# Splitting the next output's weights ahead of the finished output's epilogue in a split-precision GEMM, with other PSUM banks and another mix of side work for one projection

## The chip, the core and the metric

The kernel runs on one core of a Trainium2 chip. The metric is the device time of one execution in microseconds (us), lower is better. Of several runs the median counts. A core has a tensor engine (PE, its weight loads are listed as PEld), a vector engine (DVE), a scalar engine (ACT), GpSimd (POOL) and a sync engine (SP) that here only issues transfers. Each has its own instruction stream, and they meet at semaphores.

## The reference, cut to what matters

The reference is a two-layer backbone over 256 latent tokens with 256 context tokens ahead of them, 1024 features wide, in fp32. Layer 0 mixes tokens with a Conformer convolution, layer 1 with a bidirectional chunkwise mLSTM. Each mixer is followed by a squared-ReLU MLP, and each sub-layer ends in a layer norm of the scaled stream plus the gated result.

```python
def sq_relu_mlp(u, w1, w2):
    return jnp.square(jax.nn.relu(u @ w1)) @ w2

def conformer_conv(u, rows, w_pw1, b_pw1, w_dw, b_dw, ln_g, ln_b, w_pw2, b_pw2):
    a = u @ w_pw1 + b_pw1
    a = a[..., :CONV_DIM] * jax.nn.sigmoid(a[..., CONV_DIM:])
    ...
    a = jax.nn.silu(layer_norm(a + b_dw, ln_g, ln_b))
    return a @ w_pw2 + b_pw2

def mlstm_features(u, w_up, w_conv, b_conv, w_q, w_k, w_v, w_gate, b_gate, w_o, b_o):
    up = u @ w_up
    xm, z = up[..., :MLSTM_INNER], up[..., MLSTM_INNER:]
    xc = jax.nn.silu(dwconv(xm, w_conv) + b_conv)
    q, k, v = xc @ w_q, xc @ w_k, xm @ w_v
    ...
```

Only latents need z, the gate half of the up projection: 16 outputs of 128 features by 256 tokens.

## The kernel before

Activations lie feature-major: a tile holds 128 features by 512 tokens, context in the first 256 columns (LO) and latents in the last 256 (HI). An fp32 product is built from two fp32r parts of each operand. For each 128x1024 block of weights, which is one output of 128 features (over 1024 input features), `split_w` makes the high part `wh` on ACT (a CAST at L154) and the low part `wl` on DVE (a subtraction at L155). `mm3` then issues three matmuls per block of 128 input features: wh by the high part of the activations (L177), wh by the low part (L180) and wl by the high part (L181), 24 per output. There are four buffers each of `wh` and `wl`, and three raw buffers (L148 to L151) that SP fills with 1 MB loads, two blocks in each.

`gemm_steps` (L209) is the loop over outputs for most projections: pw1 of the Conformer, most of both MLPs, up_x and up_z of the mLSTM, and others. Outputs come in groups of two that share a raw buffer. With `ko`, the first `ko` outputs are interleaved over the eight blocks of input features, since their activations arrive one by one. For the rest, a group takes both its PSUM banks at once, and then for each output splits the weights, issues the matmuls, calls the epilogue `epi`, and yields so that a caller may put other work between. PSUM has three banks with tag "mm", two "ln", one "fl" and two "cv".

The order in which the text issues instructions is not the final one. A scheduler sorts them by their dependences, the pools' buffers and its own estimates, with the text's order as priority, and writes one fixed stream for each engine. ACT's stream also holds the issues of several transfers to DRAM.

Three callers matter below. The first is pw1, whose epilogue `pw1_epi` (L648 to L660) makes a sigmoid on ACT (gate outputs) or a product on DVE (L655), four transposes on PE (L658) and a copy. During pw1, DVE also reduces rows of the modulation weights (the ISA instructions at L379, the products L766 and L768), and the Conformer's convolution runs in `spectral`: transforms on PE (L675, L680) into two "mm" banks, four products each on DVE (L690, L691), inverse transforms (L701) into a "cv" bank, and L708 and L709 behind them.

The second is z. Its epilogue `z_epi` (L1011 to L1015) is a sigmoid on ACT (L1013), a product on DVE that reads the bank too (L1014), and the issue of a transfer to `zs_dr` on ACT's stream (L1015). The outputs are interleaved with two side generators, one step per output: `u1_half(0)` makes the context half of the normalised activations `u` in eight steps (DVE L493, L494 and L516, ACT L515), and `rows` makes token-major rows of the latents in four (DVE L1029 into two `E` buffers, PE transposes L1035, ACT copies L1037). The `E` buffers, four in all, also hold z's epilogue results until their transfers are done.

The third is the v projection of the mLSTM after up_x, in which matmuls of v (weights wv) stand beside the folding of the gate weights: L812 multiplies raw wqT tiles straight from their raw buffers, so both kinds of loads go through the same three raw buffers and SP's stream.

Of the kernel before, what the change touches and what calls it, by code (L numbers as in the profile page):

```python
# [17 lines left out]
DT = D // P  # L18
# [4 lines left out]
C = 256  # L23
# [49 lines left out]
def hybrid_kernel(ctx: ExitStack, tc: tile.TileContext, xT, vecs_d, rows_d, wdw_d, ada0_w, ada_w, adar_w, wg_d, pw1a, pw1, pw2, w1_0, w2_0,  # L73
# [132 lines left out]
        for _ in gemm_steps(*a, **k):  # L206
            pass

    def gemm_steps(w_ap, groups, rhs, n, epi, ko=0, pre=None, mm=mm3):  # L209


        if isinstance(rhs, dict):
            parts = [(LO, rhs[0]), (HI, rhs[1])]
        else:
            parts = [(slice(0, n), rhs)]
        kh_n = len(parts[0][1]) // 8
        groups = list(groups)
        pre = pre or {}
        raws = {}
        if ko:  # L220
            ws, pss = [], []
            for m in range(ko):
                g = groups[m // 2]
                if m not in pre:
                    if g not in raws:
                        raws[g] = raw_load(w_ap[g, 0])
                    pre[m] = split_w(raws[g][:, (m % 2) * 1024:(m % 2 + 1) * 1024])
                ws.append(pre[m])
                pss.append(psum("mm" if m < 3 else "cv")[:, :n])
            for kt in range(8):  # L230
                for m in range(ko):
                    mm3(pss[m], *kcol(ws[m], kt), *rhs[kt], kt == 0, kt == 7)
            for m in range(ko):
                epi(m, pss[m])
        for gi, g in enumerate(groups):
            if 2 * gi + 1 < ko:
                continue
            ms = [m for m in (0, 1) if 2 * gi + m >= ko]
            pss = {m: psum()[:, :n] for m in ms}
            for kh in range(kh_n):  # L240
                raw = raws.get(g)
                for m in ms:
                    w = pre.get((g, kh, m))
                    if w is None:
                        if raw is None:
                            raw = raw_load(w_ap[g, kh])
                        w = split_w(raw[:, m * 1024:(m + 1) * 1024])
                    for sl, r in parts:
                        for kt in range(8):
                            mm(pss[m][:, sl], *kcol(w, kt), *r[kh * 8 + kt], kh == 0 and kt == 0,  # L250
                                kh == kh_n - 1 and kt == 7)
                    if kh == kh_n - 1:
                        epi(gi * 2 + m, pss[m])
                    yield

    def gemm2(*a, **k):
        for _ in gemm2_steps(*a, **k):
# [640 lines left out]
    side = silu(1)  # L898
# [5 lines left out]
    def mlp(w1, w2, uu, res, n, g2, feed, hmake, after, each1=None, each=None, keep=None, pre=None):  # L904

        def part(c):
            hid = {}

            def e1(m, ps, s=None, sl=slice(0, n)):
                r, q = tmp("E")[:, :ps.shape[-1]], tmp("E")[:, :ps.shape[-1]]  # L910
                nc.scalar.activation(r, ps, AF.Relu)
                nc.vector.tensor_tensor(q, r, r, op=ALU.mult)
                if m not in hid:
                    if n == T:
                        hid[m] = hmake(F32R), hmake(F32R)
                    else:
                        t = hmake(F32R)
                        hid[m] = t[:, :n], t[:, n:2 * n]
                split(hid[m][0][:, sl], hid[m][1][:, sl], q)
                if each1:  # L920
                    each1(c, m, s)

            groups = range(4 * c, 4 * c + 4)
            if keep and c == 0:
                gemm2(w1, groups[:3], uu, HALVES, e1, keep, ko=3)
                gemm(w1, groups[3:], uu, n, lambda m, ps: e1(m + 6, ps))
            else:
                gemm(w1, groups, uu, n, e1, ko=0 if c else 3 + Z.pre4 if pre else 3, pre=pre if c == 0 else None)
            after(c)

            def e2(m, ps, s=None, sl=slice(0, n)):
                for s_, g, sl_ in g2:
                    if s is None or s == s_:
                        p_ = ps if s is not None else ps[:, sl_]
                        nc.vector.scalar_tensor_tensor(res[m][:, sl_], p_, g[:, m:m + 1], res[m][:, sl_],
                                                       op0=ALU.mult, op1=ALU.add)
                if c == 3:
                    feed(m, s)
                if each:
                    each(c, m, s)  # L940

            hs = [hid[i] for i in range(8)]
            if keep and c == 3:
                gemm2(w2[c], range(4), hs, HALVES[::-1], e2, keep)
            else:
                gemm(w2[c], range(4), hs, n, e2, ko=Z.kw2)

        for c in range(4):
            part(c)
# [89 lines left out]

    side = u1_half(0)  # L1040
    side2 = rows()
    for i, _ in enumerate(gemm_steps(up_z, range(8), [(h_[:, HI], l_[:, HI]) for h_, l_ in u1], C, z_epi, ko=3)):
        next(side if i < DT else side2, None)
    for s_ in (side, side2):
        for _ in s_:
            pass
# [721 lines left out]
```

## Time and profile before

| what | value |
|---|---|
| runs | 1692.59, 1693.88, 1698.11 us, median 1693.88 |
| profiled execution | 1694.68 us |
| span of its trace | 1693.0 us, so 1.68 us lie around it |
| PE busy | 1661.1 us (98% of the span) |
| DVE busy | 1092.0 us (65%) |
| ACT busy | 745.7 us (44%) |
| POOL busy | 33.4 us (2%) |
| mean granted TensorE clock | 0.995 |

Rows of the timeline give the start in the span, the duration, the engine, the line, the operation, output and input; a bracket at the end holds the idle time before the instruction and what ended it. ACTq and SPq rows are issues of transfers. A row with "x3" stands for three instructions in a run. A row of stretches gives, for each engine, busy time and the number of instructions, then the granted clock of PE, the DMA engines' busy share and GB/s. Durations of PE matmuls overlap, so the time that an output takes is read from the starts.

### The profile page before, as it was taken

To read this page: it belongs to the slowest core of one execution; us is meant where nothing else is said; L and a number is where in the kernel's file an instruction comes from. 1 tells how busy PE (TensorE), PEld (TensorE's weight loads), DVE (VectorE), ACT (ScalarE), POOL (GpSimd) and SP (SyncE) were. 2 spreads that over 40 slices of the span, in tenths; PEclk is the share of its full clock that TensorE was granted. 3 is DMA by queue.
4 is the path that set the end of the run, shared out by engine and by line. 5 is a ranking of instruction groups with operands and counts; after the bars stand their busy time and mean duration, and the time that the engine had idled before them with its cause. 6 is when DMAs were issued, how large, how long until landed. Compare 5 with 4: busy or idle time off the path is not lost.

```text
span 1693.0 us, 22721 instructions
## 1 busy us (share of the span) xinstructions
PE 1661.1 (98%) x8853; PEld 1366.3 (81%) x8853; DVE 1092.0 (65%) x1964; ACT 745.7 (44%) x1206; POOL 33.4 (2%) x84
## 2 busy tenths in 40 slices
PE   8998999999999999999999999999999999999998
PEld 5754997888888998876688899888877878888886
DVE  7995897876666776763132543453387786678765
ACT  3322763232324465542232532442376674555652
POOL 0000000000000000000000000000011110000000
PEclk9999999999999999999999999999999999999999
DMA  9534216565554054568653642344355555645651
GB/s 386 210 130 160 102 57 225 199 222 199 199 195 178 26 183 158 190 217 274 239 191 101 219 150 100 104 171 144 119 187 198 187 188 212 242 172 218 240 186 47
DMA packets 60668, 301.60 MB, mean 178 GB/s; under 512 B 6066, under 2 KB 20946, under 8 KB 27152
## 3 DMA queue, kind: packets, MB, share of 16 engines
q1 hardware_dynamic: 42832, 285.44, 46.7%
q10 hardware_dynamic: 17728, 14.70, 2.7%
q8 instruction: 70, 1.15, 0.3%
q14 instruction: 38, 0.31, 0.1%
HBM read 284.37 MB, written 15.75 MB: 177 GB/s over the span
## 4 chain that ended last, share of the span: by engine, by line
PE 91%; DVE 5%; ACT 2%; issue 1%; DMA 1%; POOL 0%; SPq 0%; DVEq 0%; ACTq 0%; POOLq 0%
PE mm L177 17%; PE mm L180 17%; PE mm L181 17%; PE mm L192 4%; PE mm L187 3%; PE mm L185 3%; PE mm L1591 3%; PE mm L186 3%; PE mm L196 2%; PE cv L187 2%; PE cv L186 2%; PE cv L185 2%; PE mm L1592 2%; DVE wl L155 1%; PE fl L812 1%; PE ln L177 1%
## 5 line engine op out<-in xcount | busy, mean ns | idle before, releaser
L155 DVE TENSOR_TENSOR wl<-raw,wh 128x1024 fp32r<-128x1024 f32 x346 | 421.8, 1223 | 306.4 <-ACT wh L154 303.3
L154 ACT CAST wh<-raw 128x1024 fp32r<-128x1024 f32 x346 | 360.4, 1050 | 483.4 <-PE mm L180 286.3
L180 PE MATMUL mm<-u,wh 128*128 128x512 f32 (+1 forms) x848 | 301.8, 357 | 1.0 <-DVE u L525 0.6
L177 PE MATMUL mm<-u,wh 128*128 128x512 f32 (+1 forms) x720 | 253.6, 355 | 3.8 <-DVE E L1014 3.2
L181 PE MATMUL mm<-u,wl 128*128 128x512 f32 (+1 forms) x720 | 250.5, 350 | 0.5 <-DVE wl L155 0.5
L180 PEld LDWEIGHTS mm<-u,wh 128*128 128x128 f32 x848 | 161.1, 190 | 24.5 <-issue 1.8
L177 PEld LDWEIGHTS mm<-u,wh 128*128 128x128 f32 x720 | 136.1, 190 | 28.5 <-issue 5.1
L181 PEld LDWEIGHTS mm<-u,wl 128*128 128x128 f32 x720 | 136.8, 190 | 19.9 <-issue 1.4
L177 PE MATMUL mm<-xm,wh 128*128 128x512 f32 x256 | 102.8, 402 | 0.0
L185 PE MATMUL mm<-wh,xl 128*128 128x512 f32 x256 | 101.3, 397 | 0.7 <-ACT wh L154 0.5
L186 PE MATMUL mm<-wh,xl 128*128 128x512 f32 x256 | 100.4, 392 | 0.6 <-DVE xl L155 0.6
L181 PE MATMUL mm<-xm,wl 128*128 128x512 f32 x256 | 100.3, 392 | 0.0
L187 PE MATMUL mm<-wl,xl 128*128 128x512 f32 x256 | 99.6, 394 | 0.3 <-DVE wl L155 0.2
L379 DVE CUSTOM_DVE_ANT_0 raw<-raw,cb,vecs 128x1024 f32<-128x1024 f32 x64 | 81.6, 1281 | 24.1 <-DMA raw<-adar_w 23.6
L177 PE MATMUL mm<-hid,wh 128*128 128x512 f32 (+1 forms) x256 | 93.2, 364 | 0.0
L180 PE MATMUL mm<-hid,wh 128*128 128x512 f32 (+1 forms) x256 | 92.8, 363 | 0.0
L181 PE MATMUL mm<-hid,wl 128*128 128x512 f32 (+1 forms) x256 | 92.8, 363 | 0.0
L1591 PE MATMUL mm<-x,wh 128*128 128x512 f32 x224 | 78.9, 397 | 0.0
L180 PE MATMUL mm<-qq,wh 128*128 128x272 f32 x256 | 73.9, 289 | 0.0
L181 PE MATMUL mm<-qq,wl 128*128 128x272 f32 x256 | 73.5, 288 | 0.0
L177 PE MATMUL mm<-qq,wh 128*128 128x272 f32 x256 | 73.5, 288 | 0.0
L192 PE MATMUL mm<-u,wh 128*128 128x512 f32 x192 | 68.4, 398 | 0.0
(496 smaller groups left out, 3269.8 us busy)
## 6 DMA issues: line engine op xcount, KB each, us to landing
raw<-w SPq DMA_DIRECT2D x64, 1024.0 KB, 4.9
raw<-adar_w SPq DMA_DIRECT2D x32, 1024.0 KB, 4.9
raw<-wo SPq DMA_DIRECT2D x32, 1024.0 KB, 4.8
raw<-ada_w SPq DMA_DIRECT2D x16, 1024.0 KB, 7.2
raw<-wv SPq DMA_DIRECT2D x16, 1024.0 KB, 5.7
raw<-wqT SPq DMA_DIRECT2D x16, 1024.0 KB, 5.5
raw<-wq SPq DMA_DIRECT2D x16, 1024.0 KB, 4.9
raw<-wk SPq DMA_DIRECT2D x16, 1024.0 KB, 4.9
```

Source lines behind the costliest of these rows:

```text
L154: c = nc.scalar.copy(hi, src)
L155: nc.vector.tensor_tensor(lo, src, hi.bitcast(F32), op=ALU.subtract)
L177: a = nc.tensor.matmul(ps, wh, xh, start=start, stop=False)
L180: nc.tensor.matmul(ps, wh, xl, start=False, stop=False)
L181: nc.tensor.matmul(ps, wl, xh, start=False, stop=stop)
L185: nc.tensor.matmul(ps, xh, wh, start=start, stop=False)
L186: nc.tensor.matmul(ps, xl, wh, start=False, stop=False)
L187: nc.tensor.matmul(ps, xh, wl, start=False, stop=stop)
L192: nc.tensor.matmul(ps, wh, x, start=start, stop=stop)
L196: nc.tensor.matmul(ps[:, :C], wl, x[:, :C], start=False, stop=False)
L379: nc.vector.tensor_tensor_reduce(dump, w, cb[:, s, :], 1.0, vecs[:, o:o + 1], ALU.mult, ALU.add, accum_out=ada[self.l][:, m, s:s + 1])
L1591: a = lambda stop: nc.tensor.matmul(ps, wh, u2[kt], start=kt == 0, stop=stop)
```

## The change

`gemm_steps` now works through a flat list of tasks, one for each output (or half of its input features). `prepare(i)` loads and splits the weights of task i. A task's weights are prepared, its bank is taken when it starts (one bank at a time, no longer two for a group), its matmuls are issued, then the next task's weights are prepared, and only then comes the epilogue. Behind a `ko` block, two tasks are prepared ahead of the block's epilogues. A new argument `banks` names the tags of the `ko` outputs' banks. Three callers change: z takes two "cv" banks and one "mm" bank for its first three outputs instead of three "mm"; z's side work takes one step of `rows` in every third output and of `u1_half(0)` in the other two, instead of all eight steps of `u1_half(0)` first; and the last quarter of layer 0's MLP interleaves the first two outputs of its second product (`ko=2`). Lines behind the function move: L379 is L387 in the new kernel, L655 is L663, L690 is L698, L1013 is L1021.

```diff
-    def gemm_steps(w_ap, groups, rhs, n, epi, ko=0, pre=None, mm=mm3):
+    def gemm_steps(w_ap, groups, rhs, n, epi, ko=0, pre=None, mm=mm3, banks=("mm", "mm", "mm", "cv")):
...
         raws = {}
+        tasks = [(gi, g, kh, m) for gi, g in enumerate(groups) for kh in range(kh_n) for m in (0, 1) if 2 * gi + m >= ko]
+        ready, pss = {}, {}
+
+        def prepare(i):
+            if i >= len(tasks) or i in ready:
+                return
+            gi, g, kh, m = tasks[i]
+            ready[i] = pre.get((g, kh, m))
+            if ready[i] is None:
+                if (g, kh) not in raws:
+                    raws[g, kh] = raws.get(g) or raw_load(w_ap[g, kh])
+                ready[i] = split_w(raws[g, kh][:, m * 1024:(m + 1) * 1024])
+
         if ko:
...
-                pss.append(psum("mm" if m < 3 else "cv")[:, :n])
+                pss.append(psum(banks[m])[:, :n])
             for kt in range(8):
                 for m in range(ko):
                     mm3(pss[m], *kcol(ws[m], kt), *rhs[kt], kt == 0, kt == 7)
+            prepare(0)
+            prepare(1)
             for m in range(ko):
                 epi(m, pss[m])
-        for gi, g in enumerate(groups):
-            if 2 * gi + 1 < ko:
-                continue
-            ms = [m for m in (0, 1) if 2 * gi + m >= ko]
-            pss = {m: psum()[:, :n] for m in ms}
-            for kh in range(kh_n):
-                raw = raws.get(g)
-                for m in ms:
-                    w = pre.get((g, kh, m))
-                    if w is None:
-                        if raw is None:
-                            raw = raw_load(w_ap[g, kh])
-                        w = split_w(raw[:, m * 1024:(m + 1) * 1024])
-                    for sl, r in parts:
-                        for kt in range(8):
-                            mm(pss[m][:, sl], *kcol(w, kt), *r[kh * 8 + kt], kh == 0 and kt == 0,
-                                kh == kh_n - 1 and kt == 7)
-                    if kh == kh_n - 1:
-                        epi(gi * 2 + m, pss[m])
-                    yield
+            pss = {}
+        for i, (gi, g, kh, m) in enumerate(tasks):
+            prepare(i)
+            w = ready[i]
+            if kh == 0:
+                pss[m] = psum()[:, :n]
+            for sl, r in parts:
+                for kt in range(8):
+                    mm(pss[m][:, sl], *kcol(w, kt), *r[kh * 8 + kt], kh == 0 and kt == 0, kh == kh_n - 1 and kt == 7)
+            prepare(i + 1)
+            if kh == kh_n - 1:
+                epi(gi * 2 + m, pss[m])
+            yield
...
-                gemm2(w2[c], range(4), hs, HALVES[::-1], e2, keep)
+                gemm2(w2[c], range(4), hs, HALVES[::-1], e2, keep, ko=2)
...
-    for i, _ in enumerate(gemm_steps(up_z, range(8), [(h_[:, HI], l_[:, HI]) for h_, l_ in u1], C, z_epi, ko=3)):
-        next(side if i < DT else side2, None)
+    for i, _ in enumerate(gemm_steps(up_z, range(8), [(h_[:, HI], l_[:, HI]) for h_, l_ in u1], C, z_epi, ko=3, banks=("cv", "cv", "mm"))):
+        next(side2 if i % 3 == 2 else side, None)
```

What the scheduler makes of it is seen in the streams. The first place is ACT at the start of z, from the third output's sigmoid to the CAST of the sixth output's weights (counted from 0, output 5; wh_964 before, wh_961 after). The names after the arrow are the sources: mm_948 is output 2's bank, E a result of the epilogue, S and u the context's activations. Before:

```order
L1013 ACTIVATE E_951_5451<-mm_948_5370 128x256
L515 ACTIVATE u_882_4979<-x_8_143,cb_881_4970,ca_880_4969 128x256
L1015 DMA zs_dr0_5329<-E_949_5443 128x256
L1015 DMA zs_dr0_5329<-E_950_5447 128x256
L1015 DMA zs_dr0_5329<-E_951_5451 128x256
L515 ACTIVATE S_956_5490<-x_8_143,cb_881_4970,ca_880_4969 128x256
L515 ACTIVATE u_885_4987<-x_19_177,cb_881_4970,ca_880_4969 128x256
L515 ACTIVATE S_963_5532<-x_19_177,cb_881_4970,ca_880_4969 128x256
L154 CAST wh_964_5536<-raw_959_5496 128x1024
```

After:

```order
L1021 ACTIVATE E_956_5461<-mm_948_5370 128x256
L1021 ACTIVATE E_958_5490<-mm_957_5465 128x256
L523 ACTIVATE u_882_4979<-x_8_143,cb_881_4970,ca_880_4969 128x256
L1023 DMA zs_dr0_5329<-E_954_5453 128x256
L1023 DMA zs_dr0_5329<-E_955_5457 128x256
L1023 DMA zs_dr0_5329<-E_956_5461 128x256
L1023 DMA zs_dr0_5329<-E_958_5490 128x256
L523 ACTIVATE S_959_5496<-x_8_143,cb_881_4970,ca_880_4969 128x256
L154 CAST wh_961_5525<-raw_951_5447 128x1024
```

The sigmoid of output 3 (E_958) and its transfer's issue now stand ahead of output 5's CAST, and one pair of the context's activations (u_885, S_963) no longer does.

The second place is DVE at the convolution's first products in pw1 (F from the banks mm_151 to mm_159 before, mm_152 to mm_160 after; u_100 takes the inverse transform from a "cv" bank). Before:

```order
L768 TENSOR_SCALAR x_8_143<-x_8_143,gb_584 128x256
L379 ISA raw_185_922,ada0_112<-raw_185_922,cb_117,vecs_72 128x1024
L379 ISA ada0_112 128x1
L690 TENSOR_TENSOR F_153_806<-mm_152_802,H_121_629 128x512
L691 TENSOR_TENSOR F_154_807<-mm_152_802,H_122_630 128x512
L690 TENSOR_TENSOR F_155_810<-mm_151_801,H_121_629 128x512
L691 TENSOR_TENSOR F_156_811<-mm_151_801,H_122_630 128x512
L690 TENSOR_TENSOR F_160_826<-mm_159_822,H_121_629 128x512
L691 TENSOR_TENSOR F_161_827<-mm_159_822,H_122_630 128x512
L768 TENSOR_SCALAR x_19_177<-x_19_177,gb_584 128x256
L708 TENSOR_TENSOR u_100_557<-cv_157_814,bdw_625 128x512
```

After:

```order
L387 ISA raw_188_928,ada0_112<-raw_188_928,cb_117,vecs_72 128x1024
L387 ISA ada0_112 128x1
L698 TENSOR_TENSOR F_154_809<-mm_153_805,H_122_632 128x512
L699 TENSOR_TENSOR F_155_810<-mm_153_805,H_123_633 128x512
L698 TENSOR_TENSOR F_156_813<-mm_152_804,H_122_632 128x512
L699 TENSOR_TENSOR F_157_814<-mm_152_804,H_123_633 128x512
L698 TENSOR_TENSOR F_161_829<-mm_160_825,H_122_632 128x512
L699 TENSOR_TENSOR F_162_830<-mm_160_825,H_123_633 128x512
L387 ISA dump_190_933,ada0_112<-raw_188_928,cb_117,vecs_72 128x1024
L387 ISA ada0_112 128x1
L716 TENSOR_TENSOR u_100_557<-cv_158_817,bdw_628 128x512
```

One of the reductions that stood ahead of the first product stands behind the sixth, and the modulation's TENSOR_SCALARs have left this stretch.

The third place is SP's stream at the start of the v projection. Before:

```order
L150 DMA raw_1182_6820<-wv 128x2048
L150 DMA raw_1186_6851<-wqT 128x2048
L150 DMA raw_1189_6885<-wqT 128x2048
L150 DMA raw_1190_6891<-wv 128x2048
L150 DMA raw_1194_6923<-wqT 128x2048
L150 DMA raw_1200_6967<-wqT 128x2048
L150 DMA raw_1203_6975<-wv 128x2048
```

After:

```order
L150 DMA raw_1180_6818<-wv 128x2048
L150 DMA raw_1187_6854<-wqT 128x2048
L150 DMA raw_1189_6885<-wv 128x2048
L150 DMA raw_1192_6891<-wqT 128x2048
L150 DMA raw_1196_6927<-wqT 128x2048
L150 DMA raw_1197_6957<-wv 128x2048
L150 DMA raw_1203_6973<-wqT 128x2048
```

From the second pair on, each load of wv stands one load of wqT earlier.

## The prediction

> **What bounds the kernel now.** I read the page first: busy shares, the chain that ended last, the costliest groups.
>
> ```profile
> span 1693.0 us, 22721 instructions
> PE 1661.1 (98%) x8853; PEld 1366.3 (81%) x8853; DVE 1092.0 (65%) x1964; ACT 745.7 (44%) x1206; POOL 33.4 (2%) x84
> PE 91%; DVE 5%; ACT 2%; issue 1%; DMA 1%; POOL 0%; SPq 0%; DVEq 0%; ACTq 0%; POOLq 0%
> L154 ACT CAST wh<-raw 128x1024 fp32r<-128x1024 f32 x346 | 360.4, 1050 | 483.4 <-PE mm L180 286.3
> ```
>
> PE is the bound. The change removes no matmul, so it can win only what PE spends waiting or at a lower clock: 1693.0 - 1661.1 = 32 us of idle time. The row of L154 says more: a CAST takes 1.05 us, and most of ACT's idle time before CASTs (286 of 483 us) ends when PE frees a `wh` buffer. In most of the kernel ACT is ahead of PE, and the four buffers stop it. Issuing splits earlier in the text brings nothing there.
>
> Next I read PE's waits by what ended them:
>
> ```profile
> PE ln L306 <- DVE fold L139: 4.7, 1, 4.7
> PE mm L177 <- DVE E L1014: 3.2, 1, 3.2
> PE ln L743 <- ACT u L723: 3.1, 1, 3.1
> PE ln L658 <- ACT wh L154: 0.9, 1, 0.9
> PE mm L675 <- DVE F L691: 0.8, 1, 0.8
> PE ln L1035 <- DVE E L1029: 0.6, 1, 0.6
> PE mm L177 <- ACT wh L154: 0.5, 1, 0.5
> PE mm L181 <- DVE wl L155: 0.5, 1, 0.5
> ```
>
> Two of the large ones are out of reach: L306 at the start, and L743 behind the convolution's norm, whose code and order stay. L1014 and L1035 are in z, and L658, L675 and L181 in pw1; L177 behind a CAST stands at the start of a second part of an MLP's product, which the edit does not reach. So two stages decide: z (600 to 646 us) and pw1 (50 to 131 us).
>
> **z, the wait that goes.** PE, then ACT and DVE, in z's timeline:
>
> ```profile
> 601.54 0.28 PE L181 MATMUL mm<-u,wl 128*128 128x256 f32 x1
> 605.06 0.58 PE L177 MATMUL mm<-u,wh 128*128 128x256 f32 x1 [3.24 <-DVE E L1014]
> 612.27 0.28 PE L177 MATMUL mm<-u,wh 128*128 128x256 f32 x1
> 615.15 0.28 PE L177 MATMUL mm<-u,wh 128*128 128x256 f32 x1
> 600.92 1.05 ACT L154 CAST wh<-raw 128x1024 fp32r<-128x1024 f32 x1 [2.87 <-PE mm L180]
> 603.56 0.94 ACT L1013 ACTIVATE E<-mm 128x256 f32<-128x256 f32 x3
> 604.37 0.61 ACT L515 ACTIVATE u<-x,cb,ca 128x256 fp32r<-128x256 f32 x1
> 605.04 1.34 ACTq L1015 DMA_DIRECT2D zs_dr<-E  x3
> 607.92 1.04 ACT L154 CAST wh<-raw 128x1024 fp32r<-128x1024 f32 x1
> 604.59 1.08 DVE L1014 TENSOR_TENSOR E<-mm,E 128x256 f32<-128x256 f32 x3
> 608.99 1.22 DVE L155 TENSOR_TENSOR wl<-raw,wh 128x1024 fp32r<-128x1024 f32 x1 [0.17 <-ACT wh L154]
> ```
>
> Counting outputs from 0: outputs 0 to 2 hold all three "mm" banks. Output 3 starts at 605.06, when the first product at L1014 has freed one. An undisturbed output takes 615.15 - 612.27 = 2.88 us (24 starts 0.12 apart). From 605.06 to output 6 at 615.15 are 10.09 us, but three outputs need 8.64. The missing 1.45 us show in the granted clock, read in stretches of 3.41 us:
>
> ```profile
> 154.17:157.58 3.41, 1.15 (x12) 0.13 (x4) 2.92 (x16) 0.07 (x1) 0.00 (x0) 1.00 0.96 363
> 157.58:161.00 3.42, 2.61 (x8) 1.11 (x10) 2.27 (x4) 3.42 (x6) 0.00 (x0) 0.50 0.97 393
> 601.32:604.73 3.41, 0.50 (x5) 0.30 (x3) 3.30 (x9) 3.10 (x6) 0.00 (x0) 1.00 0.01 2
> 604.73:608.14 3.41, 3.08 (x14) 3.08 (x15) 3.38 (x11) 1.96 (x5) 0.00 (x0) 0.50 0.36 117
> ```
>
> After a stretch with PE busy 0.50 of 3.41 us, and after one with 1.15, the next ran at 0.50. These stretches start on one grid: (601.32 - 154.17) / 3.413 is 131.0.
>
> With two "cv" banks, output 3 finds an "mm" bank free and needs only weights that ACT cast long before. PE goes on at 601.54 + 0.12 = 601.66, and output 6 would start at 601.66 + 8.64 = 610.30, which is 4.85 us earlier (3.4 of wait, 1.45 of slow clock). That is the upper bound here.
>
> **z, the wait that comes.** Output 4's weights are no problem: the CAST at 600.92 stays, its wl is done by about 603.2, and PE wants them at 604.54. Output 5's CAST started at 607.92, and PE will now want it at 601.66 + 5.76 = 607.42. I follow ACT's new order. The first three sigmoids end at 604.50 as before. Output 3's sigmoid now stands behind them and cannot start until its matmuls end at 604.54; I take 0.3 us for the release, so 604.85 to 605.2. Then u of the context to 605.7 (these are 0.5 apart), four issues instead of three, at 1.34 / 3 = 0.45 each, to 607.5, S to 608.05, and then the CAST: 608.05 to 609.1. The subtraction takes 1.22 us more and ends at 610.35, 2.9 us after PE wanted it. Two of every three matmuls need only wh, but they alternate, so PE gains some 0.2 us from that: the new wait is 2.7 us. Queued behind the sigmoid on ACT are the side work and that CAST, and PE waits for the CAST. Net 4.85 - 2.7 = 2.15 us, if the clock stays up. Output 6 and what follows find ACT ahead again: its CAST follows 1.3 us behind.
>
> The lower bound: a new wait of 2.7 us can lower the clock too. On the grid above, the stretch with at most 1.15 us busy needs 2.26 us of the wait inside it. That holds for (3.41 - 2.7) + 2 x (2.7 - 2.26) = 1.6 of the 3.41 us of possible positions, 47%, and takes back up to 1.45 us. The position is open, since pw1 shifts z against the grid. And if ACT's queue comes 0.6 us later than I say, 0.1 us is left: 0.1 to 4.85.
>
> [...]
>
> **z, the side work.** The other wait is later:
>
> ```profile
> 635.80 0.73 DVE L1029 TENSOR_SCALAR E<-x,al 128x256 f32<-128x256 f32 x2 [1.46 <-DMA zs_dr<-E]
> 636.27 1.09 PE L1035 MATMUL ln<-ident,E 128*128 128x128 f32 x6 [0.58 <-DVE E L1029]
> ```
>
> L1029 waited for an `E` buffer that z's transfers held, and the transposes stood in PE's stream already. Mixed two to one, the rows' steps come several outputs ahead of their transposes: 0.58 us go. The context's u ends two or three outputs before up_x needs it, so I cost its delay at nothing; two outputs (5.8 us) cover it. Bounds 0 to 0.58.
>
> **pw1.** Rows of DVE and PE, and a stretch:
>
> ```profile
> 50.00:112.00 62.00, 60.55 (x244) 38.50 (x243) 59.07 (x102) 12.53 (x17) 0.00 (x0) 1.00 0.46 169
> 82.97 0.69 DVE L690 TENSOR_TENSOR F<-mm,H 128x512 f32<-128x512 f32 x1
> 84.40 1.10 PE L675 MATMUL mm<-A,ge 128*128 128x512 f32 x2 [0.83 <-DVE F L691]
> 86.54 0.69 DVE L691 TENSOR_TENSOR F<-mm,H 128x512 f32<-128x512 f32 x1 [0.49 <-PE cv L701]
> 87.14 0.34 DVE L768 TENSOR_SCALAR x<-x,gb 128x256 f32<-128x256 f32 x1
> 105.86 0.50 PE L181 MATMUL mm<-u,wl 128*128 128x512 f32 x1 [0.47 <-DVE wl L155]
> 130.58 0.63 PE L658 MATMUL ln<-ident,E 128*128 128x128 f32 x4 [0.94 <-ACT wh L154]
> ```
>
> DVE is busy 59.07 of 62.00 us, so it sets the pace beside PE, and what counts is how much of its work stands ahead of what PE waits for. The group held a bank that pw1's next output did not need yet; now it is taken later, and the convolution's transforms have three "mm" banks. Two reductions and the TENSOR_SCALARs (0.34 us each) leave the place ahead of or between the products, while a weight split moves ahead of them. Following DVE's new order, the products start about 0.4 us earlier and lose some 0.6 us less among themselves (the 0.49 at 86.54 among it): 1.0 us at the convolution's end. The split stands earlier, so the 0.47 at 105.86 goes: 1.5 us. The 0.94 at 130.58 stays: PE there waits for a product on DVE that waits for PE's own last matmul. Below: if DVE has no slack to give, 0.3. Above: all four waits, 0.83 + 0.47 + 0.94 and a smaller one, 2.4. I take 1.5, nearest to the sum of the two waits (1.3) that the order moves.
>
> What pw1 wins is passed on through the wait at L743, which follows its releaser on DVE and ACT. How the two slow stretches around it fall on the grid can move by part of one stretch, worth up to 1.45 us either way; I cost this at nothing and keep it in the range.
>
> **Elsewhere.** In the MLPs, up_x and the later projections, ACT waits for `wh` buffers (the L154 row), and PE's list has no wait for weights beyond those quoted that is longer than 0.5 us. Moving epilogues behind one split costs them 1.05 us on ACT and 1.22 on DVE, hidden by the third bank; without it each would cost that much. `ko=2` in the MLP removes no wait that the list has. Both 0, with 0.5 us either way. In the v projection one load order changes:
>
> ```profile
> 753.87 3.96 SPq L150 DMA_DIRECT2D raw<-wqT  x2
> raw<-wqT SPq DMA_DIRECT2D x16, 1024.0 KB, 5.5
> 752.74 1.06 PE L812 MATMUL fl<-raw,wgq 128*32 128x512 f32 x8
> 759.87 1.06 PE L812 MATMUL fl<-raw,wgq 128*32 128x512 f32 x8
> ```
>
> A buffer freed by L812 at 752.74 is reloaded from 753.87, lands 5.5 us later at 759.4, and is used at 759.87: 0.5 us of slack. By the new order wv takes the buffer that one L812 frees and wqT the next, with the same distance, so I take 0.
>
> **The sum.** 2.15 + 0.58 + 1.5 = 4.2 us. The profiled execution's 1694.68 becomes 1690.5. It lies 0.8 above the median of the runs, so on the median's footing 1689.7.
>
> **The rivals.**
> 1. The new wait does not come: ACT takes output 5's CAST earlier than I follow it, or output 4 is slowed so that nothing is late. For it: ACT has a table load and idle spots just there that may fall otherwise. Then 4.85 + 0.58 + 1.5 = 6.9 us, 1687.0. Against: a stream is in order, and E_958 stands ahead of that CAST. 0.2.
> 2. The wait changes its place alone: the new wait lowers the clock (2.15 - 1.45 = 0.7), and DVE in pw1 is full (0.3). With a little of the rest, 1 us: 1692.9. For it: the 47% above, and DVE's 95% in pw1. 0.27.
> 3. Slower: wqT's loads, one load further back in SP's stream, come late at L812. It decides from 0.5 us of lateness. For it: SP issues in order, and the slack is small. At 1 us late in each of eight pairs, +8 - 4.2 = +3.8, 1697.7; behind a whole second load it would be more. Against: the order by buffers above. 0.09.
>
> My forecast has 0.44. Its own range is 1687.5 to 1692.0. To hold 8 in 10, the range reaches over rivals 1 and 2 with 1.5 to 2 us for the slow stretches: 1685.0 to 1695.0. A measurement of this kernel tells apart about 0.3%, 5.1 us. Faster by more: nearly all of rival 1 and a third of the forecast, 0.35. Slower: most of rival 3 and a rest, 0.08. Within: 0.57.
>
> **What would show it.** In the changed profile: no wait for L1014 behind output 2; PE's next wait in z ended by wl or wh of output 5, 2 to 3 us long, and a full clock behind it; no wait at L1035; in pw1 no wait at the third transform, and its end 1 to 2 us earlier; PE from 660 us on as before, only shifted. Waits at L812 or of up_x for u would prove me wrong, as would a wait for weights in an MLP.

## The result, and the profile after

The changed kernel takes 1690.03 us (median of 20 runs, 1688.64 to 1692.61), the kernel before 1695.11 us (median of 20, 1692.24 to 1699.65). The ratio is 0.997, with a 95% interval of 0.9963 to 0.9977: 5.1 us faster, 0.30%. Forecast were 4.2 us. The profiled execution of the changed kernel is one of its slower ones (1691.92 us), so its span is only 2.8 us shorter than the one of before. Why, the places below show.

The page after, and the list of PE's waits:

```profile
span 1690.2 us, 22717 instructions
PE 1660.0 (98%) x8853; PEld 1366.5 (81%) x8853; DVE 1091.3 (65%) x1964; ACT 745.5 (44%) x1206; POOL 33.5 (2%) x84
PE ln L751 <- ACT u L731: 3.3, 2, 3.1
PE mm L177 <- ACT wh L154: 2.2, 2, 1.3
PE ln L666 <- DVE E L663: 1.1, 1, 1.1
PE mm L181 <- DVE wl L155: 0.8, 1, 0.8
PE mm L683 <- DVE F L699: 0.5, 1, 0.5
```

The waits for z's product (3.2 us at L1014) and for z's transposes (0.6 at L1035) are gone from the list. Waits for wh at L177 stand in their place, and one for wl.

z in the timelines of PE, ACT and DVE, and the two stretches of the clock's grid in which the new waits lie:

```profile
602.10 0.28 PE L181 MATMUL mm<-u,wl 128*128 128x256 f32 x1
602.22 0.28 PE L177 MATMUL mm<-u,wh 128*128 128x256 f32 x1
609.08 0.39 PE L177 MATMUL mm<-u,wh 128*128 128x256 f32 x1 [0.95 <-ACT wh L154]
610.34 0.39 PE L181 MATMUL mm<-u,wl 128*128 128x256 f32 x1 [0.76 <-DVE wl L155]
613.08 0.28 PE L177 MATMUL mm<-u,wh 128*128 128x256 f32 x1
605.29 0.38 ACT L1021 ACTIVATE E<-mm 128x256 f32<-128x256 f32 x1 [0.24 <-PE mm L181]
605.57 0.59 ACT L523 ACTIVATE u<-x,cb,ca 128x256 fp32r<-128x256 f32 x1
605.60 1.84 ACTq L1023 DMA_DIRECT2D zs_dr<-E  x4
607.49 0.60 ACT L523 ACTIVATE S<-x,cb,ca 128x256 f32<-128x256 f32 x1 [1.32 <-DVE x L501]
608.00 1.03 ACT L154 CAST wh<-raw 128x1024 fp32r<-128x1024 f32 x1
606.46:609.87 3.41, 2.18 (x16) 1.76 (x15) 3.34 (x9) 2.38 (x5) 0.00 (x0) 1.00 0.46 153
609.87:613.28 3.41, 2.94 (x24) 2.94 (x25) 3.41 (x7) 2.81 (x4) 0.00 (x0) 1.00 0.49 137
```

PE runs from the interleaved outputs into output 3 without a break (602.10, 602.22). Output 5 then waits 0.95 us for its CAST and 0.76 for its subtraction, and the clock stays at 1.00. From the last interleaved matmul to output 6 it was 615.15 - 601.54 = 13.61 us before, and is 613.08 - 602.10 = 10.98 now: 2.63 us won. In ACT's rows, four issues take 1.84 us between the sigmoid of output 3 and S; the CAST follows.

pw1, from a full set of 16 folded rows at its start (first row) over the first matmul behind the convolution's forward transforms (second) to the first matmul of the next product (third), and a place some 38 us further on (fourth). The first four rows are of the kernel before, the others of the change:

```profile
24.56 1.07 PE L319 MATMUL fl<-raw,cs 128*32 128x256 f32 x16
95.60 0.50 PE L177 MATMUL mm<-u,wh 128*128 128x512 f32 x1
130.97 0.36 PE L177 MATMUL mm<-u,wh 128*128 128x256 f32 x1
169.40 1.05 PE L327 MATMUL fl<-fold,F 128*128 128x4 f32 x8
...
25.14 1.07 PE L327 MATMUL fl<-raw,cs 128*32 128x256 f32 x16
95.67 0.50 PE L177 MATMUL mm<-u,wh 128*128 128x512 f32 x1
130.21 0.36 PE L177 MATMUL mm<-u,wh 128*128 128x256 f32 x1
167.76 1.05 PE L335 MATMUL fl<-fold,F 128*128 128x4 f32 x8
```

106.41 us became 105.07: 1.34 us won, 0.51 of them up to the second row. With z's 2.63 and what z's transposes and its end bring (1.0 us up to up_x), these are 5.0 us, near the 5.1 by which the medians differ.

The two traces differ in other places too, so this sum is not the whole account. The change is 0.58 us late at the first row, and it wins 0.88 us between the third and the fourth. There, behind the wait at L743, one stretch runs at half clock (159.31 to 162.72), where the kernel before has two (157.58 to 164.41). And at 266.71 PE waits for a CAST, and the next stretch runs at half clock: 0.76 us more of wait than before and 1.6 of slow clock. Together these 2.4 us hide about half of the gain in the profiled execution (a matmul at 249.18 before starts at 247.59 now, a later one at 279.24 starts at 280.01). The first ACT row is the change's CAST, the second that of the kernel before:

```profile
266.71 0.50 PE L177 MATMUL mm<-u,wh 128*128 128x512 f32 x1 [1.28 <-ACT wh L154]
265.13:268.54 3.41, 2.13 (x16) 1.69 (x13) 2.82 (x4) 1.99 (x2) 0.00 (x0) 1.00 0.81 293
268.54:271.95 3.41, 3.41 (x10) 2.63 (x9) 2.03 (x4) 1.99 (x2) 0.00 (x0) 0.50 0.99 394
265.62 1.99 ACT L154 CAST wh<-raw 128x1024 fp32r<-128x1024 f32 x2 [0.66 <-DMA raw<-w]
...
266.46 1.99 ACT L154 CAST wh<-raw 128x1024 fp32r<-128x1024 f32 x2
```

Before, the same place waited 0.52 us and kept its clock, and its CAST did not wait for the load.

### The profile page after: what moved, and what is told of

Read it like the earlier page. It is cut to its first block, busy times and chain, and to the rows that moved or that the text cites. A ratio compares the mean times of both kernels' runs of the same rounds, so it can differ in the third digit from the quotient of the medians.

```text
span 1690.2 us, 22717 instructions
## 1 busy us (share of the span) xinstructions
PE 1660.0 (98%) x8853; PEld 1366.5 (81%) x8853; DVE 1091.3 (65%) x1964; ACT 745.5 (44%) x1206; POOL 33.5 (2%) x84
## 3 DMA queue, kind: packets, MB, share of 16 engines
q8 instruction: 70, 1.15, 0.3%
## 4 chain that ended last, share of the span: by engine, by line
PE 88%; DVE 7%; ACT 3%; issue 1%; DMA 1%; POOL 0%; SPq 0%; DVEq 0%; ACTq 0%; POOLq 0%
PE mm L177 17%; PE mm L180 16%; PE mm L181 16%; PE mm L192 4%; PE mm L1599 3%; PE mm L187 3%; PE mm L185 3%; PE mm L186 3%; PE mm L196 2%; DVE wl L155 2%; PE cv L186 2%; PE cv L187 2%; PE cv L185 2%; PE mm L1600 2%; PE fl L820 1%
## 5 line engine op out<-in xcount | busy, mean ns | idle before, releaser
L180 PE MATMUL mm<-u,wh 128*128 128x512 f32 (+1 forms) x832 | 297.8, 359 | 1.0 <-DVE u L533 0.5
L177 PE MATMUL mm<-u,wh 128*128 128x512 f32 (+1 forms) x704 | 249.7, 357 | 2.2 <-ACT wh L154 2.2
L181 PE MATMUL mm<-u,wl 128*128 128x512 f32 (+1 forms) x704 | 246.8, 352 | 0.8 <-DVE wl L155 0.8
L180 PEld LDWEIGHTS mm<-u,wh 128*128 128x128 f32 x832 | 158.0, 190 | 24.8 <-issue 1.8
L177 PEld LDWEIGHTS mm<-u,wh 128*128 128x128 f32 x704 | 133.1, 190 | 27.2 <-issue 5.1
L177 PE MATMUL mm<-xm,wh 128*128 128x512 f32 x256 | 102.8, 402 | 0.0
L387 DVE CUSTOM_DVE_ANT_0 raw<-raw,cb,vecs 128x1024 f32<-128x1024 f32 x64 | 81.5, 1280 | 28.5 <-DMA raw<-adar_w 27.9
L177 PE MATMUL mm<-hid,wh 128*128 128x512 f32 (+1 forms) x256 | 93.2, 364 | 0.0
L177 PE MATMUL mm<-qq,wh 128*128 128x272 f32 x256 | 73.5, 288 | 0.0
```

Source lines behind the costliest of these rows:

```text
L177: a = nc.tensor.matmul(ps, wh, xh, start=start, stop=False)
L180: nc.tensor.matmul(ps, wh, xl, start=False, stop=False)
L181: nc.tensor.matmul(ps, wl, xh, start=False, stop=stop)
L387: nc.vector.tensor_tensor_reduce(dump, w, cb[:, s, :], 1.0, vecs[:, o:o + 1], ALU.mult, ALU.add, accum_out=ada[self.l][:, m, s:s + 1])
```

## The experiments

All ratios are against the kernel before, run on the same chip beside them. Its median was 1695.21 us beside z's call alone, the rewrite alone and the runs without the banks and without the mix. It was 1695.52 beside those without the early split, without `ko=2`, with the issues on SP and with three tasks ahead, 1695.3 beside the one with both banks at once and the first two versions of the last part, and 1694.44 beside the last version. Line numbers move by a few between these kernels.

### One part alone: z's call, and the rewrite

z's call without the new loop (the old `gemm_steps` only gets the argument `banks`):

```diff
-                pss.append(psum("mm" if m < 3 else "cv")[:, :n])
+                pss.append(psum(banks[m])[:, :n])
...
-    ... C, z_epi, ko=3)):
-        next(side if i < DT else side2, None)
+    ... C, z_epi, ko=3, banks=("cv", "cv", "mm"))):
+        next(side2 if i % 3 == 2 else side, None)
```

> The kernel before with the new call of z alone (two cv banks, side work two to one); gemm_steps keeps its old body, with the argument for the banks. Theory (the gain of about 5 us is made of z's start, z's transposes and pw1, and z's start needs the early split as well as the banks): in ACT's stream output 5's CAST now stands behind output 4's sigmoid, so the wait for the bank (3.24 us) goes, but a wait of about 4 us for output 5's weights comes; with the transposes' 0.6 us the gain is about 1 us. Rival (the call of z is all of it): about 5 us faster, as the whole change. Second rival (the rewrite does it everywhere): no gain.

Measured: 1695.5 us, ratio 1.0003 (0.9994 to 1.0011): nothing won. PE's rows in z and two stretches:

```profile
610.28 0.39 PE L177 MATMUL mm<-u,wh 128*128 128x256 f32 x1 [2.49 <-ACT wh L154]
611.23 0.39 PE L177 MATMUL mm<-u,wh 128*128 128x256 f32 x1 [0.44 <-ACT wh L154]
612.00 0.58 PE L181 MATMUL mm<-u,wl 128*128 128x256 f32 x1 [0.27 <-DVE wl L155]
608.35:611.76 3.41, 1.01 (x4) 0.59 (x4) 3.22 (x8) 3.41 (x6) 0.00 (x0) 1.00 0.11 38
611.76:615.17 3.41, 3.17 (x15) 3.17 (x16) 3.23 (x6) 3.41 (x6) 0.00 (x0) 0.50 0.59 197
```

The banks removed the old wait, and 3.2 us of new ones with a stretch at half clock took its place. The transposes' wait is gone from this trace too, but what is left is under what the runs can tell. The first rival falls: the call is not all of it. The second forecast the number, no gain, but the trace shows why there is none: the call does move z's waits, and what it wins it loses again.

The rewrite alone (the change without `banks`, without the mix and without `ko=2`):

```diff
-    ... C, z_epi, ko=3, banks=("cv", "cv", "mm"))):
-        next(side2 if i % 3 == 2 else side, None)
+    ... C, z_epi, ko=3)):
+        next(side if i < DT else side2, None)
...
-                gemm2(w2[c], range(4), hs, HALVES[::-1], e2, keep, ko=2)
+                gemm2(w2[c], range(4), hs, HALVES[::-1], e2, keep)
```

> The new gemm_steps alone: z keeps its mm banks and its old side order, the MLP keeps no ko. Theory: pw1 gains 1.5 us, z keeps its waits for the bank (3.2 us) and at the transposes (0.6 us); in all 1.5 us faster, to 2.5 if z's later splits gain a little. Rival (earlier splits pay everywhere, above all in the MLPs): 4 to 5 us faster. Rival (z is all): no difference.

Measured: 1692.78 us, ratio 0.9983 (0.9974 to 0.9992), 2.4 us faster. Its list of PE's waits still has z's bank, and no wait at the rows' transposes:

```profile
PE mm L177 <- DVE E L1022: 3.2, 1, 3.2
```

So the transposes' wait goes without the mix. The two parts alone give 0 and 2.4 us, together 5.1: z's call pays only with the rewrite.

### One part undone

Without the banks (the first hunk above alone, the other way round):

```diff
-    ... C, z_epi, ko=3, banks=("cv", "cv", "mm"))):
+    ... C, z_epi, ko=3)):
```

> The whole change, but z's first three outputs take three mm banks again. Theory: PE waits for L1022's first product again, 3.2 us, probably with a stretch at half clock behind it, and output 5's weights are ready by then; the start of z loses the 2.8 us that the trace of the change shows there, so 2 to 2.5 us faster than before. Rival (the banks are hidden behind the weights' wait anyway, the early split does it): 4 to 5 us faster, as the whole change.

Measured: 1692.15 us, ratio 0.9982 (0.9973 to 0.9991), 3.1 us faster than before, a little more than the 2 to 2.5 expected. PE waits 3.25 us for L1022 again, and the trace has the stretch at half clock behind it (603.4 to 606.8). The banks are worth 2 us of the whole, about the 2.6 that z's rows showed.

Without the mix:

```diff
-        next(side2 if i % 3 == 2 else side, None)
+        next(side if i < DT else side2, None)
```

> The whole change, but z's side work in the old order (all eight steps of the context's u first). Theory: only the wait at the rows' transposes comes back, 0.6 us; 4.5 us faster than before. Rival (the mix is what lightens ACT at the start of z): output 5's weights come as late as without the banks' change, and 2 to 3 us of the gain are lost.

Measured: 1689.97 us, ratio 0.9975 (0.9966 to 0.9984), 5.2 us faster by the medians. z's waits are 0.95 and 0.76 us as in the change, and no wait at L1043 came back. The mix is worth nothing that these runs can tell.

Without the early split (each task is split when it starts, banks one at a time, z's new call):

```diff
-            prepare(0)
-            prepare(1)
             for m in range(ko):
                 epi(m, pss[m])
...
-            prepare(i + 1)
             if kh == kh_n - 1:
```

> The whole change, but each task's weights are split when the task starts, behind the epilogue before it (no prepare(i + 1), no prepare ahead of the first epilogues); banks are still taken one at a time, z has its new call and order. Theory: z's start is as in the run with z's call alone (a wait of about 3 us for output 5's weights and a lowered clock, net 0.4 us worse than before), the transposes still give 0.7 us; in pw1 the bank alone gives 1.0 of the 1.5 us. In all about 1.3 us faster than before. Rival (in pw1 the early split is what pays): pw1 gives nothing, no difference from before. Rival (the banks are all): 4 to 5 us faster.

Measured: 1694.95 us, ratio 0.9996 (0.9987 to 1.0005). In pw1 every wait is as before, the first two rows below; the third and fourth are ACT's in z:

```profile
84.35 1.10 PE L680 MATMUL mm<-A,ge 128*128 128x512 f32 x2 [0.83 <-DVE F L696]
105.79 0.50 PE L181 MATMUL mm<-u,wl 128*128 128x512 f32 x1 [0.47 <-DVE wl L155]
610.34 0.38 ACT L1018 ACTIVATE E<-mm 128x256 f32<-128x256 f32 x1
611.65 1.99 ACT L154 CAST wh<-raw 128x1024 fp32r<-128x1024 f32 x2
```

Between the same two matmuls as above, pw1 takes 130.91 - 24.52 = 106.39 us, as before the change (106.41). Here I was wrong: I had given the later bank 1.0 of pw1's 1.5 us. It gives nothing, and DVE's stream in pw1 is row for row the one of before. In z, output 5's CAST stands behind output 4's sigmoid again, as with z's call alone. The early split carries most of the change.

To see whether pw1 needs the bank beside the split, a group takes both its banks at its first task again, and the early splits stay:

```diff
+        got = set()
...
-            if kh == 0:
-                pss[m] = psum()[:, :n]
+            if kh == 0 and (gi, m) not in got:
+                for m_ in (0, 1):
+                    if 2 * gi + m_ >= ko:
+                        got.add((gi, m_))
+                        pss[m_] = psum()[:, :n]
```

> The whole change, but a group takes both its banks at its first task again, as before the change; the early splits stay. Theory, as it stands after the run without early splits (there pw1 kept its waits, although banks were taken one at a time): the early split and the order that it leads the scheduler to are all of pw1's gain; no difference from the change, 5 us faster than before. Rival (pw1 needs both, the convolution's third bank is what saves): the wait at the third transform grows to 0.8 us, and 1 to 1.5 us of pw1's gain are lost: 3.5 to 4 us.

Measured: 1689.55 us, ratio 0.9968 (0.9956 to 0.998), 5.8 us faster than before, and 0.57 us of wait at the third transform, where the change has 0.51. pw1 takes 130.13 - 25.05 = 105.08 us, as in the change (105.07). The bank taken one at a time is worth nothing; the early split, with the order of DVE that comes with it, is pw1's gain.

Without `ko=2` in the MLP:

```diff
-                gemm2(w2[c], range(4), hs, HALVES[::-1], e2, keep, ko=2)
+                gemm2(w2[c], range(4), hs, HALVES[::-1], e2, keep)
```

> The whole change without ko=2 in the MLP's last quarter. Theory: no difference from the change, 5 us faster than before. Rival (the interleaving hides a late hid): a wait in PE near 545 us and up to 1 us lost.

Measured: 1690.38 us, ratio 0.9971 (0.996 to 0.9983), 5.1 us faster than before: no difference from the change that these runs can tell. The traces show a small one: over 300 matmuls around the second product, the change takes 571.23 - 529.35 = 41.88 us, and this kernel takes 569.58 - 527.49 = 42.09 (before 570.67 - 528.57 = 42.10).

### What sets the new wait

z's first four transfers are issued on SP:

```diff
-        nc.scalar.dma_start(zs_dr[m // 4][:, m % 4, :], sg[:, C:])
+        (nc.sync if m < 4 else nc.scalar).dma_start(zs_dr[m // 4][:, m % 4, :], sg[:, C:])
```

> The whole change, and the transfers of z's first four outputs are issued on SP instead of ACT. Theory (ACT's in-order stream sets when output 5's weights come; four issues take 1.84 us of it): output 5's CAST starts 1.3 to 1.8 us earlier, the new wait of 1.7 us shrinks to 0 to 0.4 us, and the kernel is 6 to 6.8 us faster than before. Rival (issues cost ACT nothing, the wait is set by S's source on DVE, as the bracket in ACT's timeline says): no difference from the change, 5 us. Rival (SP's loads of weights get stuck behind the transfers): a wait for raw buffers in z, less than 5 us.

Measured: 1688.94 us, ratio 0.9966 (0.9953 to 0.9978), 6.6 us faster than before; against the change's own interval that is not clear of it, but the trace is:

```profile
606.14 0.38 ACT L1021 ACTIVATE E<-mm 128x256 f32<-128x256 f32 x1 [0.24 <-PE mm L181]
606.92 0.59 ACT L523 ACTIVATE S<-x,cb,ca 128x256 f32<-128x256 f32 x1
607.41 1.04 ACT L154 CAST wh<-raw 128x1024 fp32r<-128x1024 f32 x1
609.82 0.39 PE L181 MATMUL mm<-u,wl 128*128 128x256 f32 x1 [0.59 <-DVE wl L155]
```

From output 3's sigmoid to the CAST it is 1.27 us, where the change has 608.00 - 605.29 = 2.71, and PE's wait falls from 1.71 to 0.59 us. The bracket at S in the change (1.32 us idle, ended by x of L501 on DVE) names an engine that had long been done: with the issues away, S follows u without a gap. The issues held ACT.

Three tasks prepared ahead of z's first epilogues instead of two (a new argument `ahead`, 2 elsewhere):

```diff
-            prepare(0)
-            prepare(1)
+            for i in range(ahead):
+                prepare(i)
...
-    ... C, z_epi, ko=3, banks=("cv", "cv", "mm"))):
+    ... C, z_epi, ko=3, banks=("cv", "cv", "mm"), ahead=3)):
```

> The whole change, and z prepares three tasks ahead of the first epilogues instead of two, so that output 5's CAST stands ahead of the sigmoids. Theory: no wait for output 5's weights; but output 6's CAST now stands behind output 4's sigmoid, two S and u and a transfer, as output 5's did with z's call alone, so PE waits there instead, 1 to 1.5 us: 5.3 to 5.8 us faster than before. Rival (one CAST earlier is enough): no wait, 6.8 us faster. Rival (the sigmoids come 1 us later and the bank's wait returns): under 4.5 us.

Measured: 1692.96 us, ratio 0.9981 (0.9972 to 0.999), 2.6 us faster than before, so half the change's gain is lost, more than any of the three expected but the last, and for another reason:

```profile
608.54 0.39 ACT L1021 ACTIVATE E<-mm 128x256 f32<-128x256 f32 x1 [2.44 <-DMA zs_dr<-E]
609.81 1.03 ACT L154 CAST wh<-raw 128x1024 fp32r<-128x1024 f32 x1
610.89 0.58 PE L177 MATMUL mm<-u,wh 128*128 128x256 f32 x1 [3.46 <-ACT wh L154]
```

Output 5 no longer waits. But in the scheduler's new order output 4's sigmoid stands ahead of output 6's CAST, and it waits 2.44 us for an `E` buffer: four outputs' results hold all four until their transfers land. PE then waits 3.46 us for output 6, and two stretches run at half clock behind it (610.8 to 617.6).

### A version that beats both

With the transfers on SP, z's side work begins one output later, so that no u and S stand ahead of output 5's CAST:

```diff
-        next(side2 if i % 3 == 2 else side, None)
+        if i:
+            next(side2 if i % 3 == 0 else side, None)
```

> The change with z's first four transfers issued on SP, and z's side work begun one output later (no step behind output 3, then two of u to one of rows as before), so that output 5's CAST stands right behind output 3's sigmoid. Theory: the CAST starts 1.0 us earlier than with the transfers on SP alone, the wait of 0.6 us for its wl goes, and nothing else moves: 0.6 us faster than that kernel, about 7 us faster than before. Rival (the side work that is put off collides later: the context's u or the transposes come late): a wait in z or at up_x's start, no gain over 6.5 us.

Measured: 1688.42 us, ratio 0.9964 (0.9952 to 0.9977), 6.9 us faster than before, though one of its five runs took 1693.93. z's start has no wait left, but the rows' second transposes, which now come one output later as well, wait:

```profile
621.89 0.66 PE L1043 MATMUL ln<-ident,E 128*128 128x128 f32 x4 [1.43 <-ACT hl L1045]
```

The raw load for the last outputs of the first w1 product goes ahead of ada_w's loads, on top of that (`hook` and `raw0` are new arguments of the two loops, the second for loads already issued):

```diff
+            if i and hook:
+                hook()
...
-                gemm2(w1, groups[:3], uu, HALVES, e1, keep, ko=3)
-                gemm(w1, groups[3:], uu, n, lambda m, ps: e1(m + 6, ps))
+                raw3 = {}
+                gemm2(w1, groups[:3], uu, HALVES, e1, keep, ko=3, hook=lambda: raw3.update({(groups[3], 0): raw_load(w1[groups[3], 0])}))
+                gemm(w1, groups[3:], uu, n, lambda m, ps: e1(m + 6, ps), raw0=raw3)
```

> As the kernel before it in this call, and the raw load for the last two outputs of the first quarter's w1 product is issued when that product's second half begins, ahead of four loads of ada_w. Theory: PE's wait near 267 us (0.5 us before, 1.3 to 1.9 us in some runs, then with a stretch at half clock behind it) goes; 0.5 to 2.5 us more, so 7.5 to 9.5 us faster than before. Rival (two raw buffers are too few for ada_w's loads meanwhile): a new wait at the matmuls of ada_w (fl, L329) between 230 and 270 us, no gain.

Measured: 1689.15 us, ratio 0.9963 (0.995 to 0.9975), 6.2 us faster than before, so no further gain where 0.5 to 2.5 us were expected. The wait near 267 us is gone and ada_w's matmuls have no new one, but in this trace the transposes wait 2.04 us, with a stretch at half clock behind them (623.4 to 626.8). So the rows' steps go back to where the change has them, and only the step behind output 3 is left out:

```diff
         if i:
-            next(side2 if i % 3 == 0 else side, None)
+            next(side2 if i % 3 == 2 else side, None)
```

> As the kernel with the early w1 load and z's transfers on SP, but the steps of rows stand behind the same outputs as in the change (every third counted from output 5), and only the step behind output 3 is left out. Theory: the wait of 1.4 to 2.0 us at the rows' second transposes (behind an hl copy in ACT's stream) came with their new place and goes; no wait in z, none near 267 us; 8 us faster than before, 1687.3. Rival (the wait comes from side work being one output later at all): a wait of over 1 us at L1046 again, 6 to 7 us faster.

Measured: 1685.89 us, ratio 0.9946 (0.9931 to 0.9961), 8.6 us faster than before, 0.54%, and the fastest of all. Its longest waits in PE are those that no edit here touched:

```profile
PE ln L316 <- DVE fold L139: 4.7, 1, 4.7
PE ln L753 <- ACT u L733: 3.3, 2, 3.1
PE ln L337 <- DVE F L610: 2.1, 2, 1.5
PE fl L329 <- DMA raw<-ada_w: 1.2, 1, 1.2
```

z has no wait at all in it, from 590 to 650 us, and none stands near 267 us.

## Why the prediction was right

- **The places.** That pw1 and z win, and nothing comes from up_x and the later projections, held (`ko=2` brings 0.2 us in an MLP): 1.34 us in pw1 and 3.6 in z (2.63 at its start, 1.0 by up_x). The 0.88 us behind pw1 belong to the slow stretches around the wait at L743, which I had put at nothing and kept in the range. The three profiles without the early split (the kernel before, z's call alone, the run without it) have two such stretches there, eight of those with it have one and three have none. Whether the early split does this or the place of the grid in each execution was not separated.
- **z, the wait that goes.** Right to the tenth: output 3 follows at once, and the last version, which has no wait there, wins the upper bound of 4.85 us: between the same two matmuls, 613.35 - 595.75 = 17.60 us became 605.26 - 592.52 = 12.74.
- **z, the wait that comes.** Right in place and mechanism, the run with the issues on SP shows it, but sized at 2.7 us where the trace has 1.71 (2.2 us of lost time: 4.85 - 2.63). The term that was too large is ACT's queue. I let the issues begin when the context's u was done, 605.7; in the trace they begin with it (605.57 and 605.60), so the CAST comes some 0.6 us earlier against PE than I worked out.
- **The clock.** I put 47% on a lowered clock behind the new wait, from a stretch with 1.15 of 3.41 us busy. The profiles of the change and of three kernels whose z start has the same two waits (without the mix, without `ko=2`, both banks at once) show it lowered in one of four (without `ko=2`, from 608.63). The sum, made for the unlowered clock, stood. That the profiled execution of the change kept its clock there is luck.
- **z, the side work.** The sum's 0.58 us came, but the step that explained it is not needed. With z's call alone, which has the mix, the banks and the old loop, the wait at the transposes is gone, and it is gone with the rewrite alone as well, which has no mix. In the change without the mix it stays away. So either is enough, and the mix adds nothing to the rewrite. What in the rewrite shifts the transposes behind their `E` buffers' release, I did not isolate.
- **pw1.** 1.5 us forecast, 1.34 seen, and the mechanism half wrong: "the convolution's transforms have three banks" explains none of it, as the run without early splits shows (0.83 and 0.47 us of wait, as before) and the one with both banks at once confirms. The other half, the split's place and the order of DVE that comes with it, is all of it. The terms were off as well: 1.0 us was to come by the convolution's end and 0.5 from the split's place behind it, and the rows show 0.51 and 0.83. The wait at the third transform, which was to go, is still 0.51 us. That the sum of the two came so near is partly luck.
- **Elsewhere.** "A wait for weights in an MLP" was to prove me wrong, and one is there: 1.28 us at 266.71, where before it was 0.52. I had written that the edit does not reach it. It does run through the new loop, but the loop is not shown to lengthen the wait. In the two profiles with the old loop PE waits 0.52 us; with the new one and the load's place unchanged it is 0.52 in three and 0.87 to 1.92 in seven, the run without early splits among these (1.71). In each of those seven the CAST waits for the landing of its load, 0.25 to 1.30 us, and PE's wait is that plus 0.62. The load is not issued later in the new loop: where a CAST has no such wait it starts 7.2 us behind the issue, 266.46 - 259.28 in the kernel before and 265.03 - 257.85 without the banks, and 7.9 in the change (265.62 - 257.68). So what differs is when the load lands, and the load of the run without early splits, issued as in the old loop, lands late as well (267.75 - 259.39 = 8.4). Why it lands later in some executions stays open.
- **The rivals.** No wait at L812: wqT's loads are in time. The second rival, that the wait changes its place alone, is what z's call without the early split does.

## What to carry to other kernels

When a bank or a buffer is freed for PE, ask at once which instruction on the strict streams of ACT and DVE is late next: here banks and mix alone won nothing, since the next weights' CAST stood behind a sigmoid and PE waited 2.49 us for it, and they paid only with the split issued ahead of the epilogue. Count transfer issues as work of the engine that issues them (here 0.46 us of ACT each), above all ahead of something that PE waits for. Where a scheduler sorts the text, a small change of order can win in a place it was not meant for, and by another mechanism than the text suggests: only undoing one piece at a time tells.

## What the runs showed of the hardware

Four transfer issues held ACT for 1.84 us (0.46 us each) in the change, and an ACTIVATE that stood in front of them ran beside the first (605.57 and 605.60).

The clock was lowered behind less idle time than I had taken (3.41 - 2.13 = 1.28 us of a stretch in the change, where I took 2.26), and PE's busy share alone did not tell when. The stretches lay on one grid in each of the nine traces that have two places at half clock or more: from the start of one to that of another it is 604.73 - 157.58 = 447.15 us in the kernel before and 268.54 - 159.31 = 109.23 in the change, 131 and 32 times 3.4134. Where the clock did not change (606.46 in the change, the last two rows below), the starts are worked out from that grid. The first two rows are of the change without `ko=2`, where z's waits are 0.96 and 0.76 us, the other two of the rewrite alone, at the place near 267 us:

```profile
605.22:608.63 3.41, 1.77 (x13) 1.36 (x11) 3.34 (x9) 2.77 (x6) 0.00 (x0) 1.00 0.36 118
608.63:612.04 3.41, 3.33 (x15) 3.33 (x16) 3.41 (x7) 2.41 (x4) 0.00 (x0) 0.50 0.55 187
...
262.64:266.05 3.41, 2.04 (x18) 0.67 (x11) 2.02 (x4) 2.17 (x4) 0.00 (x0) 1.00 0.51 156
266.05:269.46 3.41, 3.41 (x21) 2.96 (x20) 1.97 (x3) 1.47 (x3) 0.00 (x0) 1.00 1.00 418
```

PE busy for 1.77 of 3.41 us (52%) was followed by a stretch at half clock, and so was 2.13 us (62%) at 265.13 in the change. But 2.04 us (60%) in the last two rows was not, and 2.18 us (64%) at 606.46 in the change was not. So no share of busy time divides the two, and what else decides is open. Near 267 us a wait of 1.28 us in the change was followed by half clock, and waits of 1.37 us (the rewrite alone) and 1.61 us (without `ko=2`) were not. In the change the slow stretch there cost about 1.6 us on top of the wait of 1.28.

The times of one kernel, which spread over 4 us for the change and 7 for the kernel before, go with the granted clock in part. Of the 74 runs of the kernel before that stand beside the experiments, the eight with a mean clock of 0.993 or 0.994 average 1697.9 us, the six with 0.998 average 1693.5. What brings the clock back is open too: after a stretch at half clock with PE busy 3.08 us it came back in the kernel before, after one with 3.09 us (610.78 to 614.19) in the kernel with three tasks ahead it did not.
